# Scaling by the row sums inside the transpose of P: a diagonal in place of the identity, and no GpSimd multiply

## The chip, the cores and the metric

The kernel runs on one core of one Trainium2 chip. The metric is the device time of one execution in microseconds, as a median of several runs. The profile is of one execution; its times are microseconds from the start of its span. TensorE is written PE (its weight loads PEld), VectorE DVE, ScalarE ACT, GpSimd POOL, and SyncE, which issues most transfers, SP.

## The reference, cut to what matters

One layer of an encoder block over 512 positions, width 2048: a modulated RMSNorm, one input projection, two token mixers on the same input (dilated windowed attention with 16 heads of 64, and chunked gated linear attention, GLA, with 4 heads), gates, an output projection, a residual and a last RMSNorm, in float32. The change lies in the attention:

```python
    s = jnp.where(mask, s + bias[None, :, None, None], NEG_INF)
    m = jnp.max(s, axis=-1, keepdims=True)
    p = jnp.exp(s - m)
    den = jnp.sum(p, axis=-1, keepdims=True)
    o = jnp.einsum('bhrnqk,bnkrhe->bhrnqe', (p / den).astype(v.dtype), vw)
    ...
    mix_w = jax.nn.softmax(jnp.stack(lses, axis=0), axis=0)
    att = jnp.einsum('pbsh,pbshe->bshe', mix_w.astype(av.dtype), jnp.stack(outs, axis=0))
```

Three patterns (window, dilation) are merged by their softmax denominators. That equals one softmax over all 512 keys whose logits carry the logarithm of the number of patterns that contain a key, and which the kernel uses: P is 512x512 per head.

## The kernel before, in words

The projection is computed in units of 512 columns (qk2, qk4, qk6, gk, gv0, ...). A unit multiplies 16 slices of the depth into four accumulators of PSUM; float32 precision comes from three products of high and low parts (lines 169 to 171, high by high, low by high or high by low). Weights arrive by DMA, ScalarE rounds them to the high part (L326), VectorE subtracts for the low part (L310). Between the matmuls of a unit TensorE carries out side work at positions given by a table (ATT_AT for attention). Units qk2, qk4, qk6 and gk carry the attention of four heads each, which were projected in the unit before. At a unit's end its accumulators are taken out into the stacked operands of the next heads (qk_evict, L557 to L569), on ScalarE and VectorE.

Attention works on tiles of 128 queries of one head, 64 tiles in all, 16 in each unit, in three items:
- score: two products into PSUM (L594, L595); VectorE adds the bias and takes the row's extreme (L598, two instructions, the second reads the accumulated value); ScalarE takes the exponential into p and the row sums into st (L601); VectorE takes the reciprocal (L602); GpSimd multiplies p by it (L603).
- turn: four transposes of 128x128 on TensorE, with p as the stationary operand and the constant identity c_ident as the moving one (L615), into PSUM; ScalarE writes the high part of the turned P (L619), VectorE the low one (L620).
- values: eight products with the values v for two tiles together (L629), then ScalarE (L632) and VectorE (L636) sum their two halves into cat.

The items come in the order score of a tile, turn of the tile before, values of the pair before that. The order on TensorE is as the code is written. On the other engines a scheduler sets the order of what each engine's queue holds; an engine works its queue off in that order. The GLA heads run later, in units gv1 to gg0; their states use small tiles with the tag stt from the same pool as the new diagonals (L775 to L792), and att (L802) is an ordinary float32 product of 128x128 tiles, with no splitting into parts. In names of tiles, st is the small tile of sums, dg the diagonal, s the scores, t the transposed P in PSUM, pt the turned P, rawv and rawg weights for column sums.

Of the kernel before, what the change touches and what calls it, by code (L numbers as in the profile page):

```python
# [10 lines left out]
F32 = mybir.dt.float32  # L11
# [3 lines left out]
ALU = mybir.AluOpType  # L15
# [3 lines left out]
P = 128  # L19
# [114 lines left out]
def block_kernel(ctx: ExitStack, tc: tile.TileContext, a: dict):  # L134
    nc = tc.nc
# [6 lines left out]
    sm = ctx.enter_context(tc.tile_pool(name="sm", bufs=4))  # L142
# [4 lines left out]
    def T2(name, dt=F32, parts=P):  # L147
        return t2.tile([parts, 512], dt, tag="t2", name=name)

    def B8(name, shape, dt=F32):  # L150
        return b8.tile([P] + shape, dt, tag="b8", name=name)
# [4 lines left out]
    def PA(name):  # L156
        return pp.tile([P, 512], F32, tag="pa", bufs=3, name=name)

    mm = nc.tensor.matmul
    tt = nc.vector.tensor_tensor  # L160
    stt = nc.vector.scalar_tensor_tensor
# [12 lines left out]
    def const(name, shape, dt=F32):  # L174
        t = cst.tile(shape, dt, tag=name, name="c_" + name)
        nc.sync.dma_start(t, a[name])
        return t
# [320 lines left out]
    for i in range(n):  # L498
        mm_task(i)
        st, k, j = chain[i]  # L500
# [15 lines left out]
    for i in range(n, 2 * n):  # L516
        mm_task(i)
        st, k, j = chain[i]
# [19 lines left out]
    ident = const("ident", [P, P])  # L538
# [35 lines left out]
    def attention(pairs):  # L574

        tiles = [(2 * p + j, i) for p in pairs for j in range(2) for i in range(4)]
        gt, pt, pr_ = {}, {}, {}
        heads = [2 * p + j for p in pairs for j in range(2)]

        def g_load(h):  # L580
            g = gp.tile([P, 896], F32, tag="g", name=f"g{h}")
            nc.sync.dma_start(g, bass.AP(grow.tensor, grow.offset + h * 1024, [[1, P], [1, 896]]))
            gt[h] = g

        def score(h, i):
            def go():
                if h % 8 == 0 and i == 0:
                    cat[h // 8] = B8(f"cat{h // 8}", [4, 512])
                if i == 1 and h != heads[-1]:
                    g_load(h + 1)  # L590
                qs, ks, kl, _ = stacks[h]
                q = slice(P * i, P * i + P)
                ps = PA(f"s{h}{i}")
                mm(ps, qs[:, q], ks, start=True, stop=False)  # L594
                mm(ps, qs[:, q], kl, start=False, stop=True)  # L595
                t = T2(f"p{h}{i}")
                st = sm.tile([P, 3], F32, tag="st", name=f"st{h}{i}", bufs=6)
                nc.vector.tensor_tensor_reduce(  # L598
                    out=t, in0=ps, in1=gt[h][:, P * i:P * i + 512], op0=ALU.add, op1=ALU.min,
                    scale=1.0, scalar=3e38, accum_out=st[:, 0:1])  # L600
                act(t, t, AF.Exp, bias=st[:, 0:1], scale=-1.0, accum_out=st[:, 1:2])  # L601
                nc.vector.reciprocal(st[:, 2:3], st[:, 1:2])  # L602
                nc.gpsimd.tensor_scalar(t, t, st[:, 2:3], 1.0, op0=ALU.mult, op1=ALU.mult)  # L603
                pr_[h, i] = t
            return go

        def turn(h, i):
            def go():
                half, ii = divmod(i, 2)
                if ii == 0:  # L610
                    pt[h, half] = B8(f"pt{h}{half}", [2, 4, 256], F32R)
                t = pr_.pop((h, i))
                pk = PA(f"t{h}{i}")
                for kt in range(4):
                    nc.tensor.transpose(pk[:, kt * P:kt * P + P], t[:, kt * P:kt * P + P], ident)  # L615
                hi = pt[h, half][:, 0, :, P * ii:P * ii + P]
                lo = pt[h, half][:, 1, :, P * ii:P * ii + P]
                src = pk.rearrange("p (k q) -> p k q", k=4)
                act(hi, src, AF.Copy)  # L619
                tt(lo, src, hi.bitcast(F32), op=ALU.subtract)  # L620
            return go

        def values(h, half):
            def go():
                t = pt.pop((h, half))
                po = PA(f"o{h}{half}")
                for kt in range(4):
                    for w in range(2):
                        mm(po[:, :256], vv[h // 4][:, kt, h % 4, :], t[:, w, kt, :],  # L629
                           start=kt == 0 and w == 0, stop=kt == 3 and w == 1)  # L630
                oh = sm.tile([64, 256], F32, tag="oh", name=f"oh{h}{half}", bufs=1)
                act(oh, po[64:128, :256], AF.Copy)  # L632
                own = stacks[h][3]
                p = h // 2
                dst = cat[p // 4][own, p % 4, 256 - 256 * half:512 - 256 * half]
                tt(dst[:, ::-1], po[0:64, :256], oh, op=ALU.add)  # L636
            return go

        items = []
        n = len(tiles)  # L640
        for x in range(n + 3):
            if x < n:
                items.append(score(*tiles[x]))
            if 1 <= x <= n:
                items.append(turn(*tiles[x - 1]))
            if 2 <= x <= n + 1 and tiles[x - 2][1] % 2 == 1:
                items.append(values(tiles[x - 2][0], tiles[x - 2][1] // 2))
        g_load(heads[0])
        start, span, move0, move1, move_last = ATT_AT
        at = [start + (q + 0.5) / len(items) * span for q in range(len(items))]  # L650
        at[0] -= move0
        at[1] -= move1
        at[-1] += move_last
        return list(zip(at, items))
# [265 lines left out]
    for n, p in (("qk2", 0), ("qk4", 2), ("qk6", 4)):  # L920
        ps = unit(n, False, attention((p, p + 1)) + ([(0.05, shift_row)] + some_sums(n) if p == 4 else []))
        for q in range(2):
            qk_evict(p + 2 + q, ps[2 * q], ps[2 * q + 1])

    ps = unit("gk", False, attention((6, 7)) + some_sums("gk"))
    gla["k"] = B8("gkt", [4, 512])
    for i in range(4):
# [244 lines left out]
```

## Time and profile before

| | |
|---|---|
| median of 3 runs | 977.16 us (976.33 to 978.8) |
| profiled execution, its span | 976.7 us |
| TensorE busy | 949.3 us, 97% |
| VectorE busy | 619.8 us, 63% |
| ScalarE busy | 436.1 us, 45% |
| GpSimd busy | 77.4 us, 8%; of this L603 46.4 us, 64 multiplies of 724 ns |
| transposes of P, L615 | 256 records, 211.6 to 475.4 us |

The profiled execution has no separate time beside its span; its span is 0.5 us below the median of the runs. Busy shares count an engine as busy when an instruction's record is open; matmul records overlap, so distances between starts say more than lengths. A row of the timeline has start, length, engine, line, operation, what it writes from what it reads, its form and count, and in brackets the idle time before it and what ended it. A row of waits has the sum, the number and the longest. A row of a group has busy time and the mean length of one in ns, then the idle time before.

### The profile page before, as it was taken

How to read it: one execution, taken by the hardware profiler on the slowest of the kernel's cores; microseconds unless marked ns; L12 is line 12 of the kernel's file. 1: busy time of each engine (PE TensorE's matmuls, PEld its weight loads, DVE VectorE, ACT ScalarE, POOL GpSimd, SP SyncE). 2: the span in 40 equal slices, each digit the busy share in tenths (PEclk: the TensorE clock that was granted, in tenths of full speed). 3: DMA queues.
4: the chain of work that ended last, by engine and by line, in shares of the span. 5: the costliest groups of instructions: out<-in, count | busy, mean ns of one | idle time of the engine just before them, and what ended most of it. 6: DMA issues, size and time to landing. Idle time of an engine off the chain costs nothing.

```text
span 976.7 us, 12006 instructions
## 1 busy us (share of the span) xinstructions
PE 949.3 (97%) x4522; PEld 782.3 (80%) x4522; DVE 619.8 (63%) x926; ACT 436.1 (45%) x731; POOL 77.4 (8%) x96
## 2 busy tenths in 40 slices
PE   8999999989999999999999999999999999999996
PEld 5888788878878777777777888888888888888886
DVE  7987899676666675776534647595885352436442
ACT  4542533565655655655413544363744151324221
POOL 0000000011111121111000000000010000203110
PEclk9999999999999999999999999999999999999998
DMA  9999487422223253432444434455465455345013
GB/s 328 411 413 369 158 324 274 132 99 77 93 84 101 86 192 103 127 107 91 135 169 162 130 108 142 139 170 176 130 220 181 141 173 192 106 132 171 22 43 130
DMA packets 42849, 159.69 MB, mean 163 GB/s; under 512 B 5252, under 2 KB 5796, under 8 KB 38056
## 3 DMA queue, kind: packets, MB, share of 16 engines
q1 hardware_dynamic: 42616, 158.61, 47.1%
q8 instruction: 35, 0.57, 0.2%
q10 hardware_dynamic: 176, 0.33, 0.1%
q14 instruction: 22, 0.18, 0.1%
HBM read 154.64 MB, written 4.28 MB: 163 GB/s over the span
## 4 chain that ended last, share of the span: by engine, by line
PE 76%; DVE 10%; DMA 5%; ACT 4%; issue 4%; POOL 1%; DVEq 0%; POOLq 0%; ACTq 0%
PE ps_o L170 6%; PE ps_o L169 6%; PE ps_o L171 6%; DMA rawg<-in_wg 4%; PE ps_qk L169 3%; PE sta L169 3%; PE stb L169 3%; PE ps_qk L171 3%; PE ps_qk L170 3%; PE stb L170 3%; PE sta L170 3%; PE stb L171 3%; PE sta L171 3%; PE ps_gv L171 3%; PE ps_gv L170 3%
## 5 line engine op out<-in xcount | busy, mean ns | idle before, releaser
L603 POOL TENSOR_SCALAR p<-p,st 128x512 f32<-128x512 f32 x64 | 46.4, 724 | 428.2 <-DVE st L602 412.7
L601 ACT ACTIVATE p<-p,st 128x512 f32<-128x512 f32 x64 | 46.1, 721 | 62.2 <-DVE st L598 62.1
L259 DVE CUSTOM_DVE_ANT_0 cb<-cb,sb,c_bcond 128x2048 f32<-128x2048 f32 (+1 forms) x32 | 73.4, 2293 | 0.1
L620 DVE TENSOR_TENSOR pt<-t,pt 128x512 fp32r<-128x512 f32 x64 | 44.1, 689 | 17.8 <-ACT pt L619 17.7
L615 PE MATMUL t<-c_ident,p 128*128 128x128 f32 x256 | 38.9, 274 | 10.0 <-POOL p L603 10.0
L615 PEld LDWEIGHTS t<-c_ident,p 128*128 128x128 f32 x256 | 30.9, 140 | 21.7 <-POOL p L603 14.9
L598 DVE CUSTOM_DVE_ANT_0 p<-s,g 128x512 f32<-128x512 f32 x64 | 43.6, 686 | 7.0 <-PE s L595 6.5
L619 ACT ACTIVATE pt<-t 128x512 fp32r<-128x512 f32 x64 | 37.9, 592 | 21.0 <-PE t L615 20.4
L259 DVE CUSTOM_DVE_ANT_0 rawg<-rawg,sb,gate 128x1024 f32<-128x1024 f32 x16 | 20.6, 1290 | 26.6 <-DMA rawg<-in_wg 26.6
L259 DVE CUSTOM_DVE_ANT_0 rawg<-rawg,sb,c_bcond 128x1024 f32<-128x1024 f32 x16 | 20.5, 1283 | 26.5 <-DMA rawg<-in_wg 26.5
L629 PEld LDWEIGHTS o<-pt,vv 128*128 128x128 f32 x256 | 34.2, 189 | 3.6 <-DVE pt L620 1.7
L629 PE MATMUL o<-pt,vv 128*128 128x256 f32 x256 | 35.9, 282 | 0.0
L1042 POOL TENSOR_TENSOR x<-x,fgain 128x512 f32<-128x512 f32 x12 | 20.3, 1697 | 184.6 <-ACT ysq L1032 184.6
L1032 ACT ACTIVATE ysq<-x 128x512 f32<-128x512 f32 (+1 forms) x17 | 10.3, 606 | 48.8 <-DVE x L1029 46.8
L602 DVE RECIPROCAL st<-st 128x1 f32<-128x1 f32 x64 | 10.4, 162 | 31.3 <-ACT p L601 31.2
L785 POOL TENSOR_SCALAR dc<-st,sc 128x256 f32<-128x256 f32 x16 | 10.5, 657 | 243.3 <-DVE st L782 238.4
L1028 DVE TENSOR_TENSOR y<-ps_o,sb 128x512 f32<-128x512 f32 (+1 forms) x17 | 11.1, 653 | 23.6 <-PE ps_o L171 23.6
L594 PE MATMUL s<-ks,qs 128*128 128x512 f32 x64 | 25.3, 396 | 0.2 <-DVE qs L558 0.2
L595 PE MATMUL s<-kl,qs 128*128 128x512 f32 x64 | 25.0, 390 | 0.0
L792 ACT ACTIVATE sq<-st,sc 128x256 f32<-128x256 f32 x24 | 12.2, 509 | 25.6 <-DVE st L787 13.5
L636 DVE TENSOR_TENSOR cat<-o,oh 64x256 f32<-64x256 f32 x32 | 13.3, 416 | 12.1 <-ACT oh L632 11.8
L632 ACT ACTIVATE oh<-o 64x256 f32<-64x256 f32 x32 | 12.2, 381 | 17.4 <-PE o L629 16.7
(1285 smaller groups left out, 2964.0 us busy)
## 6 DMA issues: line engine op xcount, KB each, us to landing
cb<-in_wm SPq DMA_DIRECT2D x31, 1024.0 KB, 10.0
rawg<-in_wg SPq DMA_DIRECT2D x32, 512.0 KB, 3.4
raw_o<-in_w_o SPq DMA_DIRECT2D x32, 512.0 KB, 3.5
raw_qk<-in_w_qk SPq DMA_DIRECT2D x24, 512.0 KB, 3.4
rawb<-in_w_sb SPq DMA_DIRECT2D x16, 512.0 KB, 5.8
rawv<-in_wv SPq DMA_DIRECT2D x16, 512.0 KB, 3.4
raw_gv<-in_w_gv SPq DMA_DIRECT2D x16, 512.0 KB, 3.4
raw_ag<-in_w_ag SPq DMA_DIRECT2D x16, 512.0 KB, 3.3
```

The source lines that it names most:

```text
L169: mm(ps, lh, rh, start=first, stop=False)
L170: mm(ps, ll, rh, start=False, stop=False)
L171: mm(ps, lh, rl, start=False, stop=last)
L259: nc.vector.tensor_tensor_reduce(out=w, in0=w, in1=with_, op0=ALU.mult, op1=ALU.add, scale=1.0, scalar=init, accum_out=dst)
L594: mm(ps, qs[:, q], ks, start=True, stop=False)
L598: nc.vector.tensor_tensor_reduce(out=t, in0=ps, in1=gt[h][:, P * i:P * i + 512], op0=ALU.add, op1=ALU.min, scale=1.0, scalar=3e38, accum_o ...
L601: act(t, t, AF.Exp, bias=st[:, 0:1], scale=-1.0, accum_out=st[:, 1:2])
L603: nc.gpsimd.tensor_scalar(t, t, st[:, 2:3], 1.0, op0=ALU.mult, op1=ALU.mult)
L615: nc.tensor.transpose(pk[:, kt * P:kt * P + P], t[:, kt * P:kt * P + P], ident)
L619: act(hi, src, AF.Copy)
L620: tt(lo, src, hi.bitcast(F32), op=ALU.subtract)
L629: mm(po[:, :256], vv[h // 4][:, kt, h % 4, :], t[:, w, kt, :], start=kt == 0 and w == 0, stop=kt == 3 and w == 1)
```

## The change

P is no longer divided on GpSimd. VectorE multiplies the identity by the reciprocals, row by row, into a diagonal dg of 128x128; the turn is four ordinary products of the undivided P with dg, which transpose and scale at once. Both operands stay float32.

```diff
+                if i % 2 == 0:
+                    diag[h, i // 2] = sm.tile([P, 256], F32, tag="stt", name=f"dg{h}{i}", bufs=2)
+                dg = diag[h, i // 2][:, P * (i % 2):P * (i % 2) + P]
...
                 nc.vector.reciprocal(st[:, 2:3], st[:, 1:2])
-                nc.gpsimd.tensor_scalar(t, t, st[:, 2:3], 1.0, op0=ALU.mult, op1=ALU.mult)
-                pr_[h, i] = t
+                nc.vector.tensor_scalar(dg, ident, st[:, 2:3], None, op0=ALU.mult)
+                pr_[h, i] = t, dg
...
-                t = pr_.pop((h, i))
+                t, dg = pr_.pop((h, i))
                 pk = PA(f"t{h}{i}")
                 for kt in range(4):
-                    nc.tensor.transpose(pk[:, kt * P:kt * P + P], t[:, kt * P:kt * P + P], ident)
+                    mm(pk[:, kt * P:kt * P + P], t[:, kt * P:kt * P + P], dg, start=True, stop=True)
```

Lines behind the change are numbered three higher in the new kernel: L598 becomes L601, the reciprocal L605, the diagonal L606, the turn L618, its high and low parts L622 and L623. TensorE's queue holds the same rows in the same order, GpSimd's loses the 64 multiplies, and SP's differs by two loads that change places (the low-rank weights and one rawv). VectorE's order changes in several places beyond the 64 new rows; three follow.

First, VectorE at the first turn of unit qk4. Before, with the split of weight qk43 ahead of the first two scores:

```order
L310 TENSOR_TENSOR qk43l<-raw_qk_2149,qk43h 128x1024
L568 TENSOR_TENSOR kl_2135<-ps_qk_3_0_1510,ks_2134 64x512
L569 TENSOR_TENSOR kl_2135<-ps_qk_3_0_1510,ks_2134 64x512
L598 ISA p_2199,st_2200<-s_2196,g_2140 128x512
L598 ISA st_2200 128x1
L598 ISA p_2214,st_2215<-s_2211,g_2140 128x512
L598 ISA st_2215 128x1
L602 RECIPROCAL st_2200<-st_2200 128x1
L602 RECIPROCAL st_2215<-st_2215 128x1
```

VectorE at the same place after:

```order
L601 ISA p_2207,st_2208<-s_2204,g_2148 128x512
L601 ISA st_2208 128x1
L310 TENSOR_TENSOR qk43l<-raw_qk_2157,qk43h 128x1024
L605 RECIPROCAL st_2208<-st_2208 128x1
L601 ISA p_2223,st_2224<-s_2220,g_2148 128x512
L601 ISA st_2224 128x1
L606 TENSOR_SCALAR dg_2209<-c_ident,st_2208 128x128
L605 RECIPROCAL st_2224<-st_2224 128x1
L606 TENSOR_SCALAR dg_2209<-c_ident,st_2224 128x128
```

The split moved from ahead of the first score to behind it, and the second score stands between the first reciprocal and its diagonal.

Second, VectorE at the tile whose turn is at 371.00 us in the trace (head 9, third tile; st_3058 before, st_3077 after). Before:

```order
L598 ISA p_3057,st_3058<-s_3054,g_2868 128x512
L598 ISA st_3058 128x1
L620 TENSOR_TENSOR pt_3022<-t_3066,pt_3022 128x4x128
L598 ISA p_3079,st_3080<-s_3076,g_2868 128x512
L598 ISA st_3080 128x1
L602 RECIPROCAL st_3058<-st_3058 128x1
L310 TENSOR_TENSOR qk66l<-raw_qk_3002,qk66h 128x1024
```

VectorE at the same tile after:

```order
L601 ISA p_3076,st_3077<-s_3073,g_2885 128x512
L601 ISA st_3077 128x1
L605 RECIPROCAL st_3077<-st_3077 128x1
L606 TENSOR_SCALAR dg_3078<-c_ident,st_3077 128x128
L623 TENSOR_TENSOR pt_3041<-t_3086,pt_3041 128x4x128
L601 ISA p_3099,st_3100<-s_3096,g_2885 128x512
L601 ISA st_3100 128x1
```

The reciprocal moved ahead of the low part of the tile before and of the next score, with the diagonal right behind it. The tile whose turn is at 441.47 us has the same difference.

Third, VectorE inside unit qk4, at the split of weight qk46. Before:

```order
L310 TENSOR_TENSOR qk46l<-raw_qk_2340,qk46h 128x1024
L602 RECIPROCAL st_2415<-st_2415 128x1
L620 TENSOR_TENSOR pt_2423<-t_2424,pt_2423 128x4x128
L636 TENSOR_TENSOR cat_1547<-o_2443,oh_2452 64x256
L598 ISA p_2461,st_2462<-s_2458,g_2345 128x512
```

VectorE at the same split after:

```order
L310 TENSOR_TENSOR qk46l<-raw_qk_2351,qk46h 128x1024
L605 RECIPROCAL st_2427<-st_2427 128x1
L623 TENSOR_TENSOR pt_2435<-t_2436,pt_2435 128x4x128
L606 TENSOR_SCALAR dg_2405<-c_ident,st_2427 128x128
L639 TENSOR_TENSOR cat_1547<-o_2455,oh_2464 64x256
```

The low part of the tile before stands between reciprocal and diagonal; five of the 64 tiles have it so.

More of the change, by code (lines that the diff above doesn't have):

```diff
@@ L576, in attention @@
         tiles = [(2 * p + j, i) for p in pairs for j in range(2) for i in range(4)]
-        gt, pt, pr_ = {}, {}, {}
+        gt, pt, pr_, diag = {}, {}, {}, {}
         heads = [2 * p + j for p in pairs for j in range(2)]
```

## Prediction

> **What bounds the kernel now.** I read the page first: the busy shares, the forty slices and the chain that ended last.
>
> ```profile
> PE 949.3 (97%) x4522; PEld 782.3 (80%) x4522; DVE 619.8 (63%) x926; ACT 436.1 (45%) x731; POOL 77.4 (8%) x96
> ...
> PEclk9999999999999999999999999999999999999998
> ...
> PE 76%; DVE 10%; DMA 5%; ACT 4%; issue 4%; POOL 1%; DVEq 0%; POOLq 0%; ACTq 0%
> ```
>
> TensorE is busy for 97% of the span at a full granted clock, and it carries 76% of the chain. GpSimd is 8% busy and has 1% of the chain. So the first question is what the edit adds to TensorE, the second how much of TensorE's remaining idle time it gives back. Both lie in the attention stretch, which I cut out by time, with the stretch behind it for comparison.
>
> ```profile
> core 0: us, PE busy (x) PEld busy (x) DVE busy (x) ACT busy (x) POOL busy (x), PEclk, DMA share, GB/s
> 195.00:482.00 287.00, 274.19 (x1430) 225.41 (x1429) 192.46 (x392) 163.25 (x311) 46.37 (x64) 1.00 0.33 107
> 482.00:740.00 258.00, 256.65 (x1253) 214.34 (x1254) 160.26 (x217) 114.50 (x187) 10.52 (x16) 1.00 0.47 154
> ```
>
> In attention TensorE idles 287 − 274.2 = 12.8 us; VectorE is busy for 192.5 of 287 us (67%), so it has room. The waits of TensorE in this stretch say whose idle time it is:
>
> ```profile
> PE t L615 <- POOL p L603: 10.0, 11, 2.9
> PE ps_qk L169 <- DVE qs L558: 1.0, 2, 0.5
> ```
>
> Eleven of the 64 turns wait for the GpSimd multiply, 10.0 us together. Everything else that TensorE waits for here is a microsecond or less. Those eleven are the only thing that this edit can give back; the timeline has them as idle time before the turn, in brackets:
>
> ```profile
> 211.58 0.66 PE L615 MATMUL t<-c_ident,p 128*128 128x128 f32 x4 [2.94 <-POOL p L603]
> 263.83 0.66 PE L615 MATMUL t<-c_ident,p 128*128 128x128 f32 x4 [0.38 <-POOL p L603]
> 280.71 0.66 PE L615 MATMUL t<-c_ident,p 128*128 128x128 f32 x4 [0.80 <-POOL p L603]
> 333.30 0.66 PE L615 MATMUL t<-c_ident,p 128*128 128x128 f32 x4 [0.71 <-POOL p L603]
> 350.19 0.66 PE L615 MATMUL t<-c_ident,p 128*128 128x128 f32 x4 [0.80 <-POOL p L603]
> 355.87 0.66 PE L615 MATMUL t<-c_ident,p 128*128 128x128 f32 x4 [0.19 <-POOL p L603]
> 371.00 0.66 PE L615 MATMUL t<-c_ident,p 128*128 128x128 f32 x4 [1.10 <-POOL p L603]
> 404.16 0.66 PE L615 MATMUL t<-c_ident,p 128*128 128x128 f32 x4 [0.38 <-POOL p L603]
> 421.07 0.66 PE L615 MATMUL t<-c_ident,p 128*128 128x128 f32 x4 [0.81 <-POOL p L603]
> 441.47 0.66 PE L615 MATMUL t<-c_ident,p 128*128 128x128 f32 x4 [1.10 <-POOL p L603]
> 475.05 0.66 PE L615 MATMUL t<-c_ident,p 128*128 128x128 f32 x4 [0.74 <-POOL p L603]
> ```
>
> Four are the first turn of a unit (211.58, 280.71, 350.19, 421.07), four the last one (263.83, 333.30, 404.16, 475.05), three lie inside.
>
> **Term 1: the product in the transpose's place (adds 29.0 us).** A busy time of records that overlap is no price; I take distances from start to start, in two stretches of TensorE's timeline: one turn with matmuls of the projection around it, and in the GLA part the products of att, which have the operand types and shapes of the new ones. The first two rows group all turns and all of att.
>
> ```profile
> L615 PE MATMUL t<-c_ident,p 128*128 128x128 f32 x256 | 38.9, 274 | 10.0 <-POOL p L603 10.0
> L802 PE MATMUL att<-qi,ki 128*128 128x128 f32 x64 | 8.0, 276 | 0.0
> ...
> 304.29 0.39 PE L171 MATMUL ps_qk<-h_lo,qk44h 128*128 128x512 f32 x1
> 304.52 0.60 PE L615 MATMUL t<-c_ident,p 128*128 128x128 f32 x4
> 304.87 0.48 PE L169 MATMUL ps_qk<-h_hi,qk44h 128*128 128x512 f32 x1
> 305.19 0.40 PE L170 MATMUL ps_qk<-h_hi,qk44l 128*128 128x512 f32 x1
> ...
> 565.42 0.39 PE L169 MATMUL ps_gv<-gv15h,h_hi 128*128 128x512 f32 x1
> 565.65 0.39 PE L170 MATMUL ps_gv<-gv15h,h_lo 128*128 128x512 f32 x1
> 565.87 0.39 PE L171 MATMUL ps_gv<-gv15l,h_hi 128*128 128x512 f32 x1
> 566.10 1.95 PE L802 MATMUL att<-qi,ki 128*128 128x128 f32 x16
> 567.80 0.48 PE L169 MATMUL ps_gv<-gv15h,h_hi 128*128 128x512 f32 x1
> 568.12 0.40 PE L170 MATMUL ps_gv<-gv15h,h_lo 128*128 128x512 f32 x1
> ```
>
> A matmul of 512 columns takes its place for 0.227 us: from 565.42 to 566.10 three of them start, in 0.68. From the start of the turn at 304.52 to the second matmul behind it at 305.19 are 0.67 us; less 0.227 for the matmul between, the four transposes took 0.443, or 0.111 each. The code asks for 256 transposes and gets 256 records; it asks for 32 products at att (four heads, two directions, four chunks) and gets 64, so a float32 product is carried out as two records. By the same measure the eight products of one head took 568.12 − 566.10 − 0.227 = 1.793 us, 0.224 each. Weight loads are inside this distance in both. The edit therefore adds 4 x 0.224 − 0.443 = 0.453 us to each turn, and 64 turns make 29.0 us. Nothing covers it: TensorE has no idle time but the 12.8 us, and the order of its queue is the same row for row, with product for transpose in 64 places.
>
> Beside that measurement stands a rule of the Trainium skill, "TensorE: Matmul & The Clock Gate", section "Terms": it says that transpose mode is 4 times faster for float32. By it a product would cost 4 x 0.111 = 0.443 us, a turn 1.33 us more, and this term would be 85 us in place of 29.0. The ratio in this trace is 2.0, not 4, on products of the very shape.
>
> **Term 2: the shorter way to the turn (gives back 7.5 us).** The old way at 280.71, with the reduction of the next score ahead of it in VectorE's queue:
>
> ```profile
> 278.67 0.08 DVE L598 DVE_READ_ACCUMULATOR2_ANT st<- 128x1 f32 x1
> 278.67 0.69 DVE L598 CUSTOM_DVE_ANT_0 p<-s,g 128x512 f32<-128x512 f32 x1
> ...
> 279.63 0.16 DVE L602 RECIPROCAL st<-st 128x1 f32<-128x1 f32 x1 [0.27 <-ACT p L601]
> 279.96 1.40 POOL L603 TENSOR_SCALAR p<-p,st 128x512 f32<-128x512 f32 x2 [16.19 <-DVE st L602]
> ```
>
> The reciprocal ended at 279.79 and the turn began at 280.71: 0.92 us for two hand-overs and the 0.70 us of one GpSimd multiply (1.40 for two). In its place comes one VectorE multiply of 128x128, directly behind the reciprocal on the same engine. No such row exists. Its bounds are the reciprocal above (128x1, 0.16 us) and these (the third row is for a rival below):
>
> ```profile
> L1063 DVE TENSOR_SCALAR x<-x,rn 128x512 f32<-128x512 f32 x4 | 1.9, 481 | 0.0
> L782 DVE TENSOR_SCALAR st<-kv,sc 128x256 f32<-128x256 f32 x8 | 3.8, 480 | 1.3 <-PE kv L775 1.1
> L620 DVE TENSOR_TENSOR pt<-t,pt 128x512 fp32r<-128x512 f32 x64 | 44.1, 689 | 17.8 <-ACT pt L619 17.7
> ```
>
> Between 0.16 and 0.48 I take 0.25, nearer the lower end: the same operation on four times the width took 0.48, and a quarter of the width on top of the reciprocal's 0.16 is 0.16 + 0.32/4 = 0.24. Over 64 turns that is 16 us of VectorE (10 to 31), which the third of its time that is idle takes up. The way shrinks from 0.92 to 0.25 + 0.05 for the hand-over, by 0.6 us (0.4 to 0.7).
>
> The eleven waits are 10.0 us of idle time; a record outlasts the start of the next by 0.39 − 0.227 = 0.16, so start to start they delay TensorE by 10.0 + 11 x 0.16 = 11.7 us. What of it goes:
> - First turns: 0.6 each, 2.4. Much of 211.58 stays (2.5 us), and 0.4 at the other three: what is late there is the score's own reduction, behind the evictions of the last projection on VectorE. At 280.71 and 350.19 the split of a weight now follows the first score instead of leading it, and the second score comes ahead of the first diagonal: the work ahead of the diagonal is the same, in another order.
> - 371.00 and 441.47: there the reciprocal stood behind the reduction of the next score, and the new order puts it and the diagonal ahead of that (0.77 us, 0.69 and 0.08 above). With the 0.6 both waits of 1.26 are gone: 2.5.
> - Last turns: 0.6 each, but no more than the wait is long: 0.54 + 0.6 + 0.54 + 0.6 = 2.3. That the turn before is longer by 0.45 helps little, since the reduction of its remainder stands in VectorE's queue ahead of this reciprocal.
> - 355.87: 0.35, all of it.
>
> Together 7.5 us, between nothing (if VectorE gets late) and 11.7.
>
> **Edits priced at nothing.** GpSimd loses 46 us of multiplies and issues no DMA, so no queue there moves; had TensorE not waited for it, its end would be worth nothing. The exponentials keep their place, and P stays undivided until the product. The diagonals share two buffers with the states of GLA; a buffer is written again two pairs of tiles later, when its turns are done. If that were late VectorE would stand, with the split of the weights queued behind. DMA on SP: the load of the low-rank weights changes places with one other load at the end of the stretch.
>
> **Sum.** The profiled execution spans 976.7 us; the median of the runs is 977.16, 0.5 more. 976.7 + 29.0 − 7.5 = 998.2 of span, 998.7 as a run's time. A measurement of this kernel can tell some 0.3%, 2.9 us.
>
> **Rivals.**
> 1. The waits decide (faster). If product and transpose cost the same, only term 2 is left: 976.7 − 7.5 + 0.5 = 969.7. For it speaks that both records last 274 and 276 ns; against it the doubled number of records and the 0.224. It turns at 0.111 + 7.5/256 = 0.140 us for a product (0.157 if all 11.7 us came back); below that the kernel is faster. That the product were still built as a transpose would end here too; the built program has it as a product with dg. 3%, and 2% for a price near the turning point, no change.
> 2. VectorE takes over the wait (1006 to 1010). In five places the new order has a subtraction of a P remainder (0.69 us, the row of L620) between reciprocal and diagonal, one shown ahead; it waits for ScalarE as well. If those turns lose their slack and no wait shrinks: 977.2 + 29.0 = 1006.2, and 5 x 0.69 = 3.5 more. Against it: VectorE's 33% idle time, and turns that come 0.45 us later each while VectorE gets 0.25 us more. 8%.
> 3. All the waits go, the first turn's too: 977.2 + 29.0 − 11.7 = 994.5. It would need the evictions ahead of the first scores to be done 2 us sooner, which nothing in the edit does. 7%.
> 4. A product takes four times a transpose, by mechanism: float32 products four passes, a transpose one. 4 x 0.111 a product, 976.7 + 85.0 − 7.5 + 0.5 = 1054.7. The att rows speak against it. This is what the Trainium skill's rule above gives. 2%.
>
> **How the numbers follow.** The forecast has 78%, by itself within 996 to 1001 (the bounds of 0.4 to 0.7 for the way, and half a microsecond for the price). Rivals 2 and 3 set the ends: 994.0 is rival 3 with the price at 0.222, 1006.2 is rival 2 without its additions. Outside remain rivals 1 and 4 and part of 2. Faster 0.03, same 0.02, slower 0.95.
>
> **What would show it.** In the new trace the turn's line has 512 records, not 256, and a turn occupies 0.89 us start to start; TensorE's busy time is about 29 us up with GpSimd's at 31. The waits before turns are some 3 to 4 us in place of 10.0, led by the first turn, and put down to VectorE. The new VectorE multiply lasts 0.16 to 0.48. I would be wrong if the new product's distance were not that of att, or if turns inside a unit waited for the diagonal.

## The result, and the profile after

The changed kernel takes 991.34 us (median of 4 runs, 989.86 to 994.71) against 977.47 us (4 runs, 976.33 to 978.8): the ratio is 1.0157, with a 95% interval of 1.0127 to 1.0187. It is slower by 13.9 us, not by the forecast 21.5; 991.3 lies below the range of 994.0 to 1006.2.

The profiled execution of the changed kernel has a span of 988.4 us and a time of 990.55. The difference of the two spans, +11.7 us, is what the traces have to explain. (The rest of the 13.9: a run of before exceeds its span by 1.8 us, so the profiled execution of before lay 1.0 us above its median; the changed kernel's lay 0.8 below; and its time exceeds its span by 0.4 more, which the last section has.) First the page of the changed kernel: the busy shares, the clock by fortieths of the span, and the chain that ended last.

```profile
PE 970.8 (98%) x4778; PEld 815.7 (83%) x4778; DVE 636.5 (64%) x990; ACT 438.8 (44%) x731; POOL 32.0 (3%) x32
...
PEclk9999999999999999999999999999999999999998
...
PE 94%; DVE 3%; ACT 1%; issue 1%; DVEq 0%
```

TensorE has 256 records more, GpSimd 64 instructions fewer, and TensorE's share of the chain went from 76% to 94%. Its idle time fell from 27.4 to 17.6 us, although the span grew. Where, shows a cut by stage, from the first matmul of one unit to the first of another: up to qk20 (no attention yet), to gv02 (the attention), to gg10 (GLA), to the end. First before, then after; the columns are busy time and number of records of each engine, then granted clock, DMA share and GB/s.

```profile
0.00:196.87 196.87, 192.27 (x801) 154.06 (x801) 165.33 (x192) 86.13 (x125) 0.20 (x4) 0.99 0.80 301
196.87:492.48 295.61, 282.42 (x1467) 231.84 (x1466) 194.44 (x394) 163.71 (x312) 46.37 (x64) 1.00 0.34 109
492.48:750.32 257.84, 256.07 (x1250) 213.71 (x1248) 164.10 (x223) 118.71 (x194) 10.52 (x16) 1.00 0.48 156
750.32:976.70 226.38, 218.52 (x1010) 182.65 (x1008) 95.90 (x119) 67.55 (x102) 20.29 (x12) 0.99 0.37 123
```

```profile
0.00:193.82 193.82, 188.58 (x801) 152.24 (x801) 165.12 (x192) 86.47 (x125) 0.20 (x4) 0.99 0.79 306
193.82:507.00 313.18, 308.71 (x1722) 266.96 (x1721) 212.07 (x459) 165.65 (x312) 0.00 (x0) 0.99 0.31 103
507.00:761.99 254.99, 254.99 (x1249) 213.81 (x1248) 163.44 (x223) 119.12 (x194) 11.48 (x16) 1.00 0.46 158
761.99:988.40 226.41, 218.52 (x1010) 182.66 (x1008) 95.87 (x119) 67.54 (x102) 20.27 (x12) 0.99 0.36 123
```

The attention grew by 17.6 us (TensorE busy +26.3, idle −8.7), where 21.5 were forecast. The two stages that the change doesn't touch shrank: the stretch ahead of it by 3.05 us, GLA by 2.85, in which TensorE now never stands still. The last stage is the same to 0.03 us.

In the attention, the groups of the new instructions, the waits of TensorE, and the timeline of the turn to which the one at 304.52 before answers:

```profile
L618 PE MATMUL t<-dg,p 128*128 128x128 f32 x512 | 68.2, 277 | 3.1 <-DVE dg L606 3.1
...
L606 DVE TENSOR_SCALAR dg<-c_ident,st 128x128 f32<-128x128 f32 x64 | 18.3, 286 | 2.0
```

```profile
PE t L618 <- DVE dg L606: 3.1, 3, 2.5
PE ps_gk L169 <- DVE qs L558: 0.5, 1, 0.5
PE plr L945 <- DVE lrs L938: 0.5, 1, 0.5
```

```profile
208.13 1.83 PE L618 MATMUL t<-dg,p 128*128 128x128 f32 x8 [2.55 <-DVE dg L606]
...
304.61 1.05 PE L618 MATMUL t<-dg,p 128*128 128x128 f32 x8
305.42 0.48 PE L169 MATMUL ps_qk<-h_hi,qk44h 128*128 128x512 f32 x1
305.73 0.40 PE L170 MATMUL ps_qk<-h_hi,qk44l 128*128 128x512 f32 x1
```

A turn has eight records and takes 305.73 − 304.61 − 0.227 = 0.893 us; eleven waits of 10.0 us became three of 3.1, of which the very first turn has 2.55. The waits of the first matmuls of qk4 and qk6 for an eviction (ps_qk behind qs: two of 1.0 us together before) are gone from the list as well; that of gk stays.

### The profile page after: what moved, and what is told of

It is laid out like the page before. It is cut to its first block, busy times and chain, and to the rows that moved or that the text cites. A ratio compares the mean times of both kernels' runs of the same rounds, so it can differ in the third digit from the quotient of the medians.

```text
span 988.4 us, 12422 instructions
## 1 busy us (share of the span) xinstructions
PE 970.8 (98%) x4778; PEld 815.7 (83%) x4778; DVE 636.5 (64%) x990; ACT 438.8 (44%) x731; POOL 32.0 (3%) x32
## 4 chain that ended last, share of the span: by engine, by line
PE 94%; DVE 3%; ACT 1%; issue 1%; DVEq 0%
PE ps_o L169 6%; PE ps_o L171 6%; PE ps_o L170 6%; PE t L618 6%; PE ps_qk L170 4%; PE ps_qk L169 4%; PE ps_qk L171 4%; PE sta L170 3%; PE sta L171 3%; PE stb L171 3%; PE ps_ag L169 3%; PE ps_gg L171 3%; PE ps_ag L171 3%; PE ps_ag L170 3%; PE ps_gg L170 3%; PE ps_gg L169 3%
## 5 line engine op out<-in xcount | busy, mean ns | idle before, releaser
L618 PEld LDWEIGHTS t<-dg,p 128*128 128x128 f32 x512 | 67.3, 192 | 9.0 <-ACT p L604 3.7
L618 PE MATMUL t<-dg,p 128*128 128x128 f32 x512 | 68.2, 277 | 3.1 <-DVE dg L606 3.1
L623 DVE TENSOR_TENSOR pt<-t,pt 128x512 fp32r<-128x512 f32 x64 | 44.0, 688 | 14.2 <-ACT pt L622 12.4
L601 DVE CUSTOM_DVE_ANT_0 p<-s,g 128x512 f32<-128x512 f32 x64 | 43.7, 685 | 9.3 <-PE s L595 9.2
L622 ACT ACTIVATE pt<-t 128x512 fp32r<-128x512 f32 x64 | 38.2, 596 | 23.3 <-PE t L618 22.6
L259 DVE CUSTOM_DVE_ANT_0 rawg<-rawg,sb,gate 128x1024 f32<-128x1024 f32 x16 | 20.5, 1283 | 22.9 <-DMA rawg<-in_wg 22.8
L605 DVE RECIPROCAL st<-st 128x1 f32<-128x1 f32 x64 | 10.4, 162 | 31.7 <-ACT p L604 31.6
L1031 DVE TENSOR_TENSOR y<-ps_o,sb 128x512 f32<-128x512 f32 (+1 forms) x17 | 11.1, 652 | 23.6 <-PE ps_o L171 23.6
L795 ACT ACTIVATE sq<-st,sc 128x256 f32<-128x256 f32 x24 | 12.2, 509 | 22.7 <-DVE st L790 11.7
L639 DVE TENSOR_TENSOR cat<-o,oh 64x256 f32<-64x256 f32 x32 | 13.3, 416 | 13.6 <-ACT oh L635 13.4
L635 ACT ACTIVATE oh<-o 64x256 f32<-64x256 f32 x32 | 12.2, 381 | 21.8 <-PE o L632 21.5
L606 DVE TENSOR_SCALAR dg<-c_ident,st 128x128 f32<-128x128 f32 x64 | 18.3, 286 | 2.0
```

Source lines behind the costliest of these rows:

```text
L259: nc.vector.tensor_tensor_reduce(out=w, in0=w, in1=with_, op0=ALU.mult, op1=ALU.add, scale=1.0, scalar=init, accum_out=dst)
L601: nc.vector.tensor_tensor_reduce(out=t, in0=ps, in1=gt[h][:, P * i:P * i + 512], op0=ALU.add, op1=ALU.min, scale=1.0, scalar=3e38, accum_o ...
L618: mm(pk[:, kt * P:kt * P + P], t[:, kt * P:kt * P + P], dg, start=True, stop=True)
```

## The experiments

The table has the attention stage of every profile, by distances from start to start on TensorE. "Turns" runs from a turn's first record to the start of the matmul behind it, "waits" from the matmul ahead of a turn to the turn, less the 0.227 us that such a matmul occupies; both are sums over 64 turns. "Projections" is the distance between two matmuls of the projection with nothing between; in it lie the waits at the start of a unit. The matmul behind a turn occupies 0.31 us instead of 0.227 in every row but that of f32r_turn; this stands under projections, so a turn counts 0.35 or 0.81 us in its column, not 0.443 or 0.893. The table leaves out the distances of the other matmuls, 86 to 89 us in each row, and the 64 times 0.227.

| kernel | stage | turns | waits | projections |
|---|---|---|---|---|
| before | 295.6 | 23.3 | 12.0 | 158.7 |
| before_again | 297.7 | 23.6 | 13.1 | 159.1 |
| after | 313.2 | 52.5 | 3.7 | 156.1 |
| again | 313.3 | 52.7 | 3.7 | 156.1 |
| product_only | 315.4 | 52.2 | 5.6 | 156.7 |
| ident_transpose | 292.1 | 23.4 | 8.1 | 158.8 |
| dve_div | 295.3 | 23.6 | 11.1 | 159.0 |
| f32r_turn | 291.7 | 26.4 | 8.5 | 153.8 |
| lag2 | 287.0 | 22.7 | 1.8 | 159.0 |
| lag2_after | 310.1 | 51.8 | 1.2 | 155.6 |

**again: the changed kernel once more**, to see what a repeat of it agrees on.

> The changed kernel once more, to see what of its profile repeats. Theory A: the change costs 64 turns x 0.43 us = 27.5 us of TensorE, and gives back about 8 us of waits before turns and 2 us at the starts of units qk4 and qk6; the 3 us that the first profile was ahead before attention began, and the 2.9 us fewer waits in the GLA part, belong to the execution and not to the change. Then the second profile reaches the first matmul of qk20 anywhere between 193 and 197 us, and the waits before go L823, gn L837 and gn L838 may be there (about 2.3 us) as before. Rival B: both belong to the change; then they repeat within 0.3 us. Ratio by A about 1.017, by B about 1.013.

990.89 us (990.52 to 996.29), 1.0153 of before (1.0123 to 1.0183), a span of 988.4 again. The profile repeats the first one nearly to the hundredth: 313.3 us of attention, 255.0 of GLA, the same three waits.

```profile
PE t L618 <- DVE dg L606: 3.1, 3, 2.6
```

So the shorter GLA and the missing waits at unit starts are no accident of one execution of the changed kernel. The start repeats as well (193.7 us), as my rival B had it; but product_only has the same order and took 196.9 us for it, and before_again, below, shows how far it moves by itself.

**product_only: the product alone.** GpSimd divides P as before; only the turn is a product with the identity.

```diff
-                    nc.tensor.transpose(pk[:, kt * P:kt * P + P], t[:, kt * P:kt * P + P], ident)
+                    mm(pk[:, kt * P:kt * P + P], t[:, kt * P:kt * P + P], ident, start=True, stop=True)
```

> The kernel before with one edit: the turn is a float32 product with the identity in place of a transpose; GpSimd still divides. Theory A: the price of the product alone, 27.5 us, less the waits that the new order on VectorE and ScalarE takes away by itself (371.00 and 441.47, 2.5 us, and 2 us at the unit starts), since the scheduler gives the same order with products whoever divides: 977 + 27.5 - 4.5 = 1000, and 9 to 10 us slower than the changed kernel at most. Rival C: the product hides in part, and the gain came from the shorter way; then it would be under 990.

995.42 us (994.25 to 999.03), 1.0193 (1.0162 to 1.0224); its span is 994.4. The price of a turn is confirmed: 52.2 − 23.3 = 28.9 us for 64 turns. But the total is up by only 18, less than I expected. The waits before turns fell from 12.0 to 5.6 us with the old, long way by GpSimd, 2.8 us came back at the projections and the other matmuls, and 2.2 in GLA:

```profile
PE t L615 <- POOL p L603: 4.8, 2, 2.9
```

Turn by turn, the waits of the last turns, those at 371.00 and 441.47 and those of the first turns of qk4 and qk6 are gone here already (0.02 us or less); left are 3.1 us at the very first turn, 2.0 at the first of gk and 0.3 at the one at 355.87. Two things can do that: the turn takes 0.45 us more of TensorE's time, in which GpSimd gets on, and the scheduler, given a product in place of a transpose, put VectorE, ScalarE and SP into just the order that they have in the changed kernel (presumably because it reckons with another cost; no run shows its reason). Most of the gain that the prediction gave to the diagonal belongs to that.

**ident_transpose: the diagonal's way alone.** The changed kernel with transposes; VectorE writes ident x reciprocal > 0, which is the identity. P stays undivided.

```diff
-                nc.vector.tensor_scalar(dg, ident, st[:, 2:3], None, op0=ALU.mult)
+                nc.vector.tensor_scalar(dg, ident, st[:, 2:3], 0.0, op0=ALU.mult, op1=ALU.is_gt)
...
-                    mm(pk[:, kt * P:kt * P + P], t[:, kt * P:kt * P + P], dg, start=True, stop=True)
+                    nc.tensor.transpose(pk[:, kt * P:kt * P + P], t[:, kt * P:kt * P + P], dg)
```

> The changed kernel with transposes: VectorE makes the identity anew from the reciprocal (multiplied, then compared with zero), so the turn waits for the same instruction as in the change, but is a transpose; P stays undivided, that part of the computation is left out. Theory A: the shorter way alone, 977 less about 8 us, 969 (967 to 972), with the turn at 0.443 us and 256 records; the waits at the starts of units qk4 and qk6 stay, since the order is that of transposes. Rival C: the product is what brought the waits down, by giving the other engines time; then this kernel gains 3 us at most.

972.49 us (968.77 to 974.09), 0.9945 (0.9925 to 0.9965): faster, by less than I expected, since 8.1 us of waits stay. VectorE's order is nearly that of before, with the diagonal in the queue. The waits, and VectorE and TensorE at the turn that began at 280.71 before:

```profile
PE t L618 <- DVE dg L606: 6.2, 10, 2.6
```

```profile
278.80 0.16 DVE L605 RECIPROCAL st<-st 128x1 f32<-128x1 f32 x1 [0.27 <-ACT p L604]
279.00 0.29 DVE L606 TENSOR_SCALAR dg<-c_ident,st 128x128 f32<-128x128 f32 x1
...
279.43 0.63 PE L618 MATMUL t<-dg,p 128*128 128x128 f32 x4 [0.35 <-DVE dg L606]
```

From the reciprocal's end at 278.96 to the turn are 0.47 us, not 0.30: 0.04 ahead of the multiply, 0.29 for it, 0.14 to TensorE. The way got 0.45 us shorter instead of 0.6. At other turns the multiply isn't right behind the reciprocal, as at a unit's last turn, where the sum into cat (L639) stands between, and the wait of 0.38 stays at 0.30:

```profile
262.01 0.16 DVE L605 RECIPROCAL st<-st 128x1 f32<-128x1 f32 x1
262.20 0.42 DVE L639 TENSOR_TENSOR cat<-o,oh 64x256 f32<-64x256 f32 x1
262.65 0.28 DVE L606 TENSOR_SCALAR dg<-c_ident,st 128x128 f32<-128x128 f32 x1
...
263.08 0.41 PE L618 MATMUL t<-dg,p 128*128 128x128 f32 x2 [0.30 <-DVE dg L606]
```

So the two halves apart: the way alone takes the waits from 12.0 to 8.1, the product alone to 5.6, both together to 3.7.

**dve_div: the division on VectorE**, as another way to do without GpSimd, with transposes.

```diff
-                nc.gpsimd.tensor_scalar(t, t, st[:, 2:3], 1.0, op0=ALU.mult, op1=ALU.mult)
+                nc.vector.tensor_scalar(t, t, st[:, 2:3], None, op0=ALU.mult)
```

> The kernel before with GpSimd's multiply of 128x512 moved to VectorE, transposes kept. Theory A: the way from reciprocal to turn falls from 0.92 to 0.48 + 0.05 us, 0.39 less at each of eleven waits, about 4 us: 973 (970 to 976). VectorE carries 31 us more in attention, 223 of 275 us. Rival D: VectorE gets late with that, and the turns wait for it: 980 or more.

975.44 us (973.76 to 977.87), 0.9989 (0.9973 to 1.0006): no change that can be told, where I expected 973. The multiply takes 486 ns on VectorE, and 11.1 us of waits stay, where I had expected some 4 us less; ten of the eleven are now put down to VectorE. The first turns of qk4, qk6 and gk wait 0.25 us less, and the wait of 1.26 at 371.00 is gone, but a turn two tiles earlier, which did not wait before, now waits 1.56 us: its multiply stands behind a split and the low part of another tile. That is my rival D, at one turn. A hand-over less and a faster multiply are worth little while what stands ahead on VectorE stays.

**before_again: the kernel before, profiled once more.**

> The kernel before once more, for a second profile. Theory A2 (after the first four runs): the 2.9 us of waits in the GLA part belong to the kernel's own timing and repeat (go L823 1.1 us, gn L837 and L838 1.2 us, within 0.2), while the first 20 us and the stretch at 108 us depend on the phase of the granted clock and differ by up to 3 us. Rival E: the GLA waits are chance as well; then they are absent or of another size here.

974.63 us, span 972.8. The waits at turns are 11.1 us in place of 10.0, those at unit starts are the same. The difference is one turn, the first of gk (421.07 in the first profile): from start to start it waits 0.98 us there and 2.05 here. GpSimd's multiply and a column sum of VectorE (L698) at that turn, in the first profile and in this one:

```profile
420.32 0.69 POOL L603 TENSOR_SCALAR p<-p,st 128x512 f32<-128x512 f32 x1 [16.22 <-DVE st L602]
420.45 1.64 DVE L698 CUSTOM_DVE_ANT_0 rawv<-rawv,shb 128x1024 f32<-128x1024 f32 x1 [0.29 <-DMA rawv<-in_wv]
```

```profile
417.14 1.23 DVE L698 CUSTOM_DVE_ANT_0 rawv<-rawv,shb 128x1024 f32<-128x1024 f32 x1
417.16 2.43 POOL L603 TENSOR_SCALAR p<-p,st 128x512 f32<-128x512 f32 x2 [16.20 <-DVE st L602]
```

Begun ahead of the column sum, the multiply took 0.69 us; begun just behind it, the first of the two took 1.76. In product_only it is 1.74, with the wait of 2.0 us. So the column of waits moves by 1 us between executions of one program. With the diagonal no GpSimd multiply stands there, and this turn waits 0.53 and 0.51 us in the two profiles of the changed kernel.

The profile also differs from the first in the start (192.3 us in place of 196.9) and in GLA (256.4 in place of 257.8). Waits of TensorE between 480 and 770 us, in the first profile of before and in this one:

```profile
PE go L823 <- DVE at L809: 1.0, 1, 1.0
PE plr L942 <- DVE lrs L935: 0.9, 1, 0.9
PE gn L837 <- ACT gsh L835: 0.6, 1, 0.6
PE gn L838 <- DVE gsl L836: 0.2, 1, 0.2
```

```profile
PE go L823 <- DVE at L809: 1.0, 1, 1.0
PE plr L942 <- DVE lrs L935: 0.6, 1, 0.6
```

The wait at L823 repeats and the two of gn don't. Of the 2.85 us that GLA lost with the change, 1.4 are therefore as good as chance. So is part of the attention's growth: against this profile's 297.7 us it is 15.5, not 17.6.

**f32r_turn: the new order with a turn as short as the old.** GpSimd divides; P and the identity are float32r, and the turn is four products. P is rounded by it.

```diff
-    ident = const("ident", [P, P])
+    id0 = T2("id0")[:, :P]
+    nc.sync.dma_start(id0, a["ident"])
+    idr = cst.tile([P, P], F32R, tag="idr", name="idr")
+    act(idr, id0, AF.Copy)
+    ident = idr.bitcast(F32)
...
-                t = T2(f"p{h}{i}")
+                t = T2(f"p{h}{i}", F32R)
...
-                    nc.tensor.transpose(pk[:, kt * P:kt * P + P], t[:, kt * P:kt * P + P], ident)
+                    mm(pk[:, kt * P:kt * P + P], t[:, kt * P:kt * P + P], idr, start=True, stop=True)
```

> The order of the changed kernel on VectorE, ScalarE and SP, but with a cheap turn: p and the identity are held as float32r, the turn is four float32r products, GpSimd divides. P is rounded to float32r, that part of the precision is left out. It parts the two reasons for which the product alone took the turns' waits from 12.0 to 5.6 us: the order, or the 0.43 us that every turn lasts longer. Theory F (the order did it): waits of 5 to 7 us here, none at 371 and 441 and none at unit starts in qk4 and qk6. Rival G (the longer turn did it): 10 us or more. The turn by itself 0.25 to 0.44 us, so 977 less 0 to 12 for it and less 2 to 8 for the waits: 960 to 973.

971.99 us (971.6 to 975.21), 0.9966 (0.9949 to 0.9984). Apart from the identity's load, VectorE, ScalarE and SP have the order of the changed kernel. The waits before turns are 8.5 us, between the 5 to 7 and the 10 or more that I had named, and the turns that answer to 371.00 and 441.47 still wait 0.86 and 0.74; the list, which counts idle time, has

```profile
PE t L619 <- POOL p L607: 7.0, 8, 3.0
```

So of the 6.4 us by which product_only shortened the waits, about 3.5 come with the order and about 2.9 with the longer turn (4.0, if the first turn of gk is left out, at which product_only met the slow multiply). The waits at unit starts are gone, in qk4 and qk6 as in the changed kernel: they go with the order, not with the diagonal. GLA takes 255.0 us, as there. (The matmul behind a turn starts differently here: 2.2 us stand under turns instead of projections. Set back, the row reads 24.2 and 156.0.)

**lag2: the turn one tile later.** Before, with turn and values each a tile later in the order of items, so that the way by GpSimd has a tile's time more.

```diff
-        for x in range(n + 3):
+        for x in range(n + 4):
...
-            if 1 <= x <= n:
-                items.append(turn(*tiles[x - 1]))
-            if 2 <= x <= n + 1 and tiles[x - 2][1] % 2 == 1:
-                items.append(values(tiles[x - 2][0], tiles[x - 2][1] // 2))
+            if 2 <= x <= n + 1:
+                items.append(turn(*tiles[x - 2]))
+            if 3 <= x <= n + 2 and tiles[x - 3][1] % 2 == 1:
+                items.append(values(tiles[x - 3][0], tiles[x - 3][1] // 2))
```

> The kernel before (transposes, GpSimd divides) with each turn one tile later in the side work: the turn of a tile comes after the score two tiles on, the values one tile later. Theory A2: all that the change gave back were waits of TensorE for a chain that is too long for its place; with one tile more (3 us) of cover nearly all of the 12 us of waits before turns go, at no price on TensorE: 977 less 8 to 11 us, 966 to 969. Rival H: the later turns push values and evictions past the unit's end and the waits come back there, 974 to 980.

965.43 us (964.63 to 967.94), 0.9892 (0.9871 to 0.9913): faster than both kernels, and a little better than I expected. Of eleven waits one is left:

```profile
PE t L615 <- POOL p L603: 1.3, 1, 1.3
```

GpSimd's 0.70 us a tile cost next to nothing once the turn comes later; some 2 us of new waits at values, scores and the start of gk take back little (the matmuls that the table leaves out go from 87.2 to 89.0 us).

**lag2_after: the same on the changed kernel.**

> The changed kernel with each turn one tile later, as in lag2. Both now have nearly no waits before turns, so what lies between them is the price of the products with no waits to give back. Theory A2: 64 x 0.43 = 27.5 us over lag2's 965.4, 993 (990 to 995), slower than the changed kernel's 991 by little or not at all, and some 1.6% over the kernel before. Rival C: the change costs by itself only the 14 us measured, 979.

989.86 us (988.49 to 991.35), 1.0125 (1.0093 to 1.0157); I expected 993. With next to no waits before turns in either, the change costs 24.4 us by the medians, and 22.8 by the two ratios to before, which ran beside each (975.98 and 977.40 us). The spans of the two profiles differ by 21.0, as lag2's is of the longest of its five runs: 29.1 at the turns (51.8 − 22.7), less 3.4 at the projections, 2.0 between the other matmuls of the attention, 0.5 at the turns' waits and 2.6 in GLA, plus 0.6 at the start. What is given back elsewhere than before turns is given back here too, which my 993 had left out.

## Why the prediction was right and wrong

**Term 1 held.** 29.0 us were forecast; product_only gives 28.9 and the changed kernel 29.2, of which 0.6 is the first turn, worked at a granted clock of 0.66 (the last section shows that this comes and goes in the kernel before, too). The Trainium skill ("TensorE: Matmul & The Clock Gate", section "Terms") has transpose mode 4 times faster for float32; turn against turn it is 0.893/0.443 = 2.0 here, so that rival is out. So is rival 1, by which a product costs as much as a transpose: done alone, it made the kernel slower by 18 us.

**Term 2 came out near in sum, and for other reasons.** Forecast 7.5 us, measured 12.0 − 3.7 = 8.3. By places it looks right, too: 2.75 us at the first turns of the units (2.4 forecast), 2.5 at 371.00 and 441.47 (2.5), 2.9 at the last turns (2.3), nothing at 355.87 (0.35). But all of it except 1.9 us is there in product_only, without the shorter way (and 1.5 of the 1.9 are at the first turn of gk, where GpSimd's multiply was slow), so the agreement is luck. The way became 0.47 us, not 0.30: the multiply took 286 ns instead of 250, the hand-over from VectorE 0.14 instead of 0.05. Had only the way got shorter, 3.9 us would have come back. The rest comes from the scheduler's order and from the turn itself, whose length I had said "helps little"; at the last turns no wait is left. The first turn kept 2.55 us, as forecast. Rival 2, VectorE late at the diagonals, came at one of its five places only. VectorE and TensorE at the turn that answers to 355.87, after:

```profile
361.57 0.15 DVE L605 RECIPROCAL st<-st 128x1 f32<-128x1 f32 x1
361.64 0.67 DVE L623 TENSOR_TENSOR pt<-t,pt 128x512 fp32r<-128x512 f32 x1
362.23 0.27 DVE L606 TENSOR_SCALAR dg<-c_ident,st 128x128 f32<-128x128 f32 x1
...
362.65 1.02 PE L618 MATMUL t<-dg,p 128*128 128x128 f32 x7 [0.19 <-DVE dg L606]
```

The low part stands between reciprocal and diagonal, and the wait stays at 0.35 us from start to start: a turn inside a unit that waits for its diagonal, which I had named as a sign of being wrong. Else VectorE's 18.3 us of multiplies (forecast 16) found room; it makes TensorE wait for three turns only.

**The step that failed is "Edits priced at nothing"**, and with it the sentence that those eleven waits "are the only thing that this edit can give back". I had read the order for where it touched a turn, and took the rest as neutral. In the attention 2.5 us came back at the projections; 1.8 of it are the waits at the first matmuls of qk4 and qk6. TensorE at the first of qk4's two waits and VectorE ahead of it, before, and VectorE at the same work after:

```profile
270.48 0.47 PE L169 MATMUL ps_qk<-h_hi,qk40h 128*128 128x512 f32 x1 [0.23 <-DVE kl L569]
...
267.67 1.22 DVE L310 TENSOR_TENSOR qk42l<-raw_qk,qk42h 128x1024 fp32r<-128x1024 f32 x1 [1.04 <-ACT qk42h L326]
...
269.64 0.69 DVE L569 TENSOR_TENSOR kl<-ps_qk,ks 64x512 fp32r<-64x512 f32 x1
```

```profile
272.04 0.69 DVE L569 TENSOR_TENSOR kl<-ps_qk,ks 64x512 fp32r<-64x512 f32 x1
272.77 0.69 DVE L558 SCALAR_TENSOR_TENSOR qs<-ps_qk,qs 64x512 fp32r<-64x512 f32 x1
273.49 1.23 DVE L310 TENSOR_TENSOR qk42l<-raw_qk,qk42h 128x1024 fp32r<-128x1024 f32 x1
```

Before, the split of qk42 (1.22 us, after 1.04 of waiting for ScalarE) stands ahead of the evictions that free the accumulators; after, it stands behind the first three of them. These waits are there in before, before_again, ident_transpose, dve_div and lag2, whose turns are transposes, and missing in after, again, product_only, f32r_turn and lag2_after, whose turns are products; product_only and f32r_turn have the order of the changed kernel with the old way. Another 0.4 each came back at the low-rank products and the one matmul of the shift. In all the attention gave back 29.2 − 17.6 = 11.6 us, as much as rival 3 had named, but only 8.3 of it at the turns.

**Outside the attention** I had put nothing. GLA shrank by 2.85 us; 1.4 of it holds against before_again. The wait at L823, 1.1 us start to start, is in both profiles of before and in none of the changed kernel. It waits for at (L809), which VectorE makes right behind a column sum that itself waits for a transfer of rawg. In the five profiles whose turn is a product (f32r_turn's among them) GLA takes 255.0 to 255.7 us, in the others 256.4 to 257.9, except dve_div with 255.2. But ident_transpose and dve_div have no wait at L823 with an order nearly that of before, and product_only has 0.6 us of it with the new one. That wait of VectorE for rawg is 2.97 us in before, 3.72 in before_again and 2.90 in product_only, and 1.45 to 2.70 in the profiles without a wait at L823; lag2, with 2.07, has one of 1.5 us all the same. So it goes in the main with the length of that wait. Why that is shorter after the change stays open; no run isolates it. The 3.05 us of the start are no part of the change, as the last section shows.

Against the forecast 21.5 stand, then, +11.7 in this pair of profiles: 3.9 us of the difference from the attention, 2.85 from GLA, 3.05 from the start. TensorE's busy time rose by 21.5 us and not by 29, since it fell by 3.7 at the start, by 1.1 in GLA, and by some 3 within the attention. Against the second profile of before the spans differ by 15.6 us: 15.5 in the attention, −1.4 in GLA, 1.5 at the start. Chance moves either difference by some us; the shortfall in the attention is in both. The direction was safe, as the price of a product stood in the trace; the size was not.

## What to carry to other kernels

Price an operation on the bounding engine by distances from start to start in rows of the same shape: that term held to 0.2 us. But where a scheduler orders the other queues, an edit of one kind of step can re-order them everywhere, so compare the whole order, what stands ahead of each wait of the bounding engine above all, not just the places next to the edit. And if the bounding engine waits for a chain on other engines, let the consumer come later before making the chain shorter with work on the bounding engine: one tile of lag won 10.6 us (0.9892), the diagonal lost 14.

## What the runs showed of the hardware that I had not expected

- One record of 128x128 with its weight load took the same 0.11 us in all three kinds of turn. Four float32 transposes took 0.443 us, eight records of float32 products 0.893, and four float32r products:

```profile
305.11 0.56 PE L619 MATMUL t<-idr,p 128*128 128x128 f32 x4
305.50 0.45 PE L169 MATMUL ps_qk<-h_hi,qk44h 128*128 128x512 f32 x1
305.79 0.40 PE L170 MATMUL ps_qk<-h_hi,qk44l 128*128 128x512 f32 x1
```

  That is 305.79 − 305.11 − 0.227 = 0.453 us, 0.113 each: a float32r product turned P no faster than a transpose.

- The start differs between executions of one kernel by several us. Up to the first matmul of qk20 it took 196.9 us in the first profile of before and 192.3 in the second. 3.2 of these 4.6 us lie in the first 20 us, where the matmuls of sta start 0.43 us apart in the first profile and 0.23 in the second, though the profile gives the clock as 1.00 for both; no run shows why. The other 1.4 lie behind a wait of TensorE for ScalarE (stb behind h_hi, L392) of 2.05 us, which both profiles have. In the first, the granted clock behind it was 0.57; first the row of before, then one of before_again around the same work:

```profile
108.00:112.00 4.00, 3.92 (x10) 3.02 (x11) 4.00 (x6) 1.76 (x4) 0.00 (x0) 0.57 0.59 209
```

```profile
104.00:108.00 4.00, 3.17 (x13) 2.32 (x14) 4.00 (x4) 2.24 (x4) 0.00 (x0) 1.00 0.68 272
```

  The same happened behind the wait of the first turn, of 2.55 us in the changed kernel and of 2.94 in before_again, and not in the first profile of before, also behind one of 2.94. The rows of after, before_again and before:

```profile
208.00:213.00 5.00, 4.87 (x21) 4.34 (x22) 2.09 (x6) 2.04 (x5) 0.00 (x0) 0.66 0.01 3
```

```profile
206.00:211.00 5.00, 4.01 (x14) 3.35 (x15) 1.73 (x6) 2.31 (x4) 1.39 (x2) 0.66 0.02 3
```

```profile
211.50:216.50 5.00, 4.92 (x26) 4.12 (x27) 3.44 (x7) 2.96 (x5) 1.42 (x3) 1.00 0.09 12
```

  The Trainium skill ("TensorE: Matmul & The Clock Gate", Part 1) says that the gate looks at windows of 3.4 us that run freely, whatever the kernel does. Such a difference between repeats agrees with that; the waits named here are all shorter than such a window, and no run measures it.

- The time of a run exceeds its span by 1.73 to 1.85 us in the kernels whose GpSimd multiplies within the attention, and by 2.0 to 2.2 in those where it doesn't. I have no explanation; it is 0.4 of the 13.9 us.
